# One sum of the experts' rows in memory split into two, with four row buffers

## The chip, the cores and the metric

The kernel runs on one core of one Trainium2 chip. A core has five engines that run side by side, each through its own list of instructions in order: PE (matrix products), DVE (VectorE, elementwise on whole tiles), ACT (ScalarE), POOL (GpSimd) and SP (which here only issues transfers). Sixteen DMA engines move data between the memory of the chip and the on-chip buffers; a transfer is issued by one of the engines into that engine's queue and reports its landing by a semaphore. The metric is the time of one execution on the device in microseconds.

## The reference

Two transformer blocks over 512 rows of 1024 numbers. The first ends in a mixture of 64 experts, of which a router picks eight for each row; a shared expert sees every row. What matters here:

```
scores = sigmoid(t @ router_w);  top_i = the 8 experts of a row;  top_w = their weights
x1     = x + gate1 * mixer(...)                    # residual, 512 x 1024
routed = sum over a row's experts e of top_w[e] * (silu(g) * u) @ w_dn[e],  [g, u] = t @ w_gu[e]
shared = (silu(g) * u) @ w_sh_dn
x2     = x1 + g2 * (routed + shared)               # g2: a gate per column
out    = second_block(rmsnorm(x2) * final_g, ...)
```

All is in 32-bit floats; `x2` is the sum that this change is about.

## The kernel before

The kernel is one class whose phases follow each other: A and B (the first block's mixer), C (the experts), D (the second block). Weights are streamed from memory: each of the 64 experts has 2 MB of up-projection in two pieces of 1 MB (`load_gu`) and 1 MB of down-projection (`load_dn`), issued by SP. Weights are split on the chip into a high part (ACT, line 166, `whi`) and a low part (DVE, line 167, `wlo`), and each product is made of three matmuls (lines 160 to 162).

Phase C first picks the experts of each row on DVE, and from these, by small matmuls, lists of row numbers (`iidx`) and weights (`widx`) for each expert. The experts are taken in a fixed order of slots, each with a fixed number of rows, `CAP[n]`: the first three have 128, then large and small ones take turns (88, 36, 88, 36 down to 68, 64), then come fourteen of up to 128, ending with 96, 96, 92, 92, 88 and 28. Rows beyond a slot's number would go through `overflow`, which runs only when there are some.

The loop in `phase_c` (line 1167 on) does for slot n: load the weights; turn the gathered rows (`ring`, four buffers) on PE, split them into `th` and `tl`, and multiply them (`routed_up`); gather the rows of slot n+4 by a transfer on POOL's queue (`gather`, line 1199); multiply slot n-1 by its down-projection (`routed_down`): eight matmuls, two `ps_dn` banks of 512 columns, then DVE multiplies by `g2` into a row buffer `ey` (line 1326), and POOL issues the scatter (line 1327), a transfer that adds each row of `ey` to its row of the sum `accd` in memory. `ey` has two buffers; the last two slots use two others (tag `th`). Transfers that add to one tensor must not overlap, so each scatter waits until the one before has landed, and a new `ey` waits until the scatter that reads its buffer has landed.

Before the loop, `shared_down` (lines 1002 to 1017) makes the shared expert's 512 x 1024 results in eight steps of 128 x 512: `sy` on DVE, then POOL adds it to the residual `x1`, and after a row block's second half POOL writes it to `accd`, which so starts as residual plus shared expert. `sy` and `ey` share two buffers.

After the loop, `moe_end` (line 1331) loads `accd` back in four transfers of 512 KB on SP (`mo`, line 1340), takes the sums of squares on ACT and the product with `final_g` on DVE (`fin`, line 1351), turns the rows on PE and makes the second block's first input (`hn`, line 1506).

The order of instructions on each engine is set when the kernel is built: a scheduler places them by its own estimate of times, together with marks in the code (`self.after(...)`), and buffers come from pools with a fixed number of each tag. The `hp` and `tok` areas that held early activations hold expert weights during the loop (n modulo 4 picks `wraw`, `hh`, `hl` or `tok`).

Of the kernel before, what the change touches and what calls it, by code (L numbers as in the profile page):

```python
# [8 lines left out]
F32 = mybir.dt.float32  # L9
# [6 lines left out]
OP = mybir.AluOpType  # L16
AX = mybir.AxisListType

S = 512
D = 1024  # L20
# [5 lines left out]
NE = 64  # L26
# [11 lines left out]
CAP = [SLOTS[r] for r in RANK]  # L38
# [103 lines left out]
class Kern:  # L142
# [859 lines left out]
    def shared_down(self):  # L1002

        nc, c = self.nc, self.cpool
        for half in range(2):
            cs = slice(half * 512, (half + 1) * 512)
            dh, dl = self.dn_piece(self.shd, half)
            for i in range(4):
                ahl = self.sha[i // 2]
                ps = self.bank("dn")  # L1010
                for k in range(2):
                    self.mm3(ps, ahl[:, 0, i % 2, k], ahl[:, 1, i % 2, k], dh[:, k], dl[:, k], k == 0, k == 1)
                y = c.tile([128, 512], F32, name="sy", tag="ey", bufs=2)
                nc.vector.tensor_tensor(y, ps, self.g2[:, cs], OP.mult)
                nc.gpsimd.tensor_tensor(self.x1[:, i, cs], self.x1[:, i, cs], y, OP.add)
                if half:
                    nc.gpsimd.dma_start(self.accd[i * 128:(i + 1) * 128, :], self.x1[:, i])

    def phase_c(self):
        nc, p, c = self.nc, self.p, self.cpool  # L1020
        hh, hl = self.hh, self.hl
        accd = self.dp.tile([S, D], F32, name="accd")
        self.mark = self.mark2 = self.mark3 = None

        self.onesb = c.tile([128, 128], BF, name="onesb")
# [14 lines left out]
        for n in range(4):  # L1040
            r = c.tile([128, D], F32, name=f"ring{n}", tag="ring", bufs=4)
# [124 lines left out]
        for n in range(NE):  # L1166
            if n % 2 == 0 and n + 6 < NE:
                with self.after(self.last):
                    self.slots(n + 6, 2, self.pos, self.RH)
            e = slice(n, n + 1) if n < FIRST else bass.ds(self.order_at(self.order[0:1, n:n + 1]), 1)  # L1170
            gu = self.load_gu(p["w_exp_gu"][0, e], n)
            dns.append(self.load_dn(p["w_exp_dn"][0, e], n))
            pg = self.routed_up(self.ring[n % 4], gu, CAP[n])
            if n + 4 < NE:
                self.gather(n + 4)
            if pend is not None:
                self.routed_down(*pend[1], dns[n - 1], self.iidx[:, n - 1:n], CAP[n - 1])
            pend = e, self.expert_act(pg, self.widx[:, n:n + 1], CAP[n], {NE - 2: "sco", NE - 1: "mk"}.get(n))
        self.routed_down(*pend[1], dns[NE - 1], self.iidx[:, NE - 1:NE], CAP[NE - 1])

        self.fin = self.raw()[:, 0:D]
        with self.after(self.loaded):
# [77 lines left out]
    def overflow(self):  # L1260

        nc, c, p, tc = self.nc, self.cpool, self.p, self.tc
        most = nc.values_load(self.cnt[0:1, 64:65], min_val=0, max_val=S)
        with tc.If(most > 0):
            with tc.For_i(0, NE, 1) as n:
                n_e = nc.values_load(self.cnt[0:1, bass.ds(n, 1)], min_val=0, max_val=S)
                with tc.If(n_e > 0):
                    e = bass.ds(self.order_at(self.order[0:1, bass.ds(n, 1)]), 1)
                    pos = c.tile([128, 4], F32, name="ovp", tag="ovp")
                    nc.vector.tensor_copy(pos, self.pos[:, :, bass.ds(n, 1)].rearrange("p i o -> p (i o)"))  # L1270
                    rh = c.tile([128, 4, 6], BF, name="ovr", tag="ovr")
                    nc.vector.tensor_copy(rh, self.RH[:, :, bass.ds(n, 1), :].rearrange("p i o n -> p (i o) n"))
                    cap = c.tile([128, 1], F32, name="ovc", tag="ovc")
                    nc.vector.tensor_copy(cap, self.cap[:, bass.ds(n, 1)])
                    nc.vector.tensor_scalar(pos, pos, cap, None, op0=OP.subtract)
                    for r in range(-(-(S - min(CAP)) // 128)):
                        if r:
                            nc.vector.tensor_scalar(pos, pos, -128.0, None, op0=OP.add)
                        ps = self.bank("sl")
                        self.slot_sums(ps[:, 0:6], pos, rh)  # L1280
                        wi = c.tile([128, 1], F32, name="ovw", tag="ovw")
                        ii = c.tile([128, 1], I32, name="ovi", tag="ovi")
                        self.slot_lists(ps, 1, wi, ii)
                        self.mark = self.mark2 = self.mark3 = None
                        gu, dn = self.load_gu(p["w_exp_gu"][0, e], 1), self.load_dn(p["w_exp_dn"][0, e], 1)
                        g = self.ring[0]
                        self.gather_rows(g, ii, 128)
                        self.routed_down(*self.expert_act(self.routed_up(g, gu, 128), wi, 128), dn, ii, 128)

    def routed_up(self, g, gu, m):  # L1290
        nc, c = self.nc, self.cpool
# [17 lines left out]
                    self.mark = mm  # L1309
        return pg  # L1310

    def routed_down(self, af, ah, al, dn, i_ap, m):
        nc, c = self.nc, self.cpool
        y = c.tile([128, D], F32, name="ey", tag="ey" if af is not None else "th", bufs=2)
        dv = dn[:].rearrange("p (k c) -> p k c", k=2)
        for half in range(2):
            cs = slice(half * 512, (half + 1) * 512)
            ps = self.bank("dn")
            if af is None:
                dh, dl = self.dn_piece(dn, half)  # L1320
                for k in range(2):
                    self.mark2 = self.mm3(ps[0:m], ah[:, k, 0:m], al[:, k, 0:m], dh[:, k], dl[:, k], k == 0, k == 1)
            else:
                for k in range(2):
                    self.mark2 = nc.tensor.matmul(ps[0:m], af[:, k, 0:m], dv[:, k, cs], start=k == 0, stop=k == 1)
            nc.vector.tensor_tensor(y[0:m, cs], ps[0:m], self.g2[0:m, cs], OP.mult)
        nc.gpsimd.indirect_dma_start(out=self.accd[:], in_=y[0:m], in_offset=None, compute_op=OP.add,
                                     out_offset=bass.IndirectOffsetOnAxis(ap=i_ap[0:m], axis=0),
                                     bounds_check=S - 1, oob_is_err=False)

    def moe_end(self, A, B):

        nc, p, d = self.nc, self.p, self.dpool
        area, fg = self.ap_.tile([128, 4, D], F32, name="fin", tag="tok"), self.fin
        ys = [self.m4.tile([128, D], F32, name="mo", tag=t, bufs=b) for t, b in (("macc", 3),) * 2 + (("mraw", 2),) * 2]
        self.xT = d.tile([128, KT, S], F32, name="xT")
        hh = self.hp.tile([128, KT, S], F32R, name="dhh", tag="hh")
        hl = self.hp.tile([128, KT, S], F32R, name="dhl", tag="hl")
        for i in range(4):
            nc.sync.dma_start(ys[i], self.accd[i * 128:(i + 1) * 128, :])  # L1340

        w = d.tile([128, 1], F32, name="sqw", tag="sqw", bufs=1)
        seq = [nc.scalar.sqrt(w, self.eps)]
# [2 lines left out]
        def sums(n):  # L1346
            y, z, i, ss = ys[n], area[:, n], n % 2, st[n // 2]
            junk = hl[:, 2 * n:2 * n + 2].rearrange("p k s -> p (k s)")
            with self.after(seq[-1]):
                seq.append(nc.scalar.activation(junk, y, AF.Square, accum_out=ss[:, i:i + 1]))  # L1350
            nc.vector.tensor_tensor(z, y, fg, OP.mult)
            with self.after(seq[-1]):
                seq.append(nc.scalar.activation(y, z, AF.Square, accum_out=ss[:, 2 + i:3 + i]))
# [34 lines left out]
        with self.tc.high_priority():  # L1388
            sums(0)
            sums(1)  # L1390
            first(0)
            turned(0)
            b0 = second(0)
            sums(2)
            sums(3)
            first(1)
            self.norm_half(0, A, B, b0[:, 0:256], hh, hl)
            with self.after(self.bcast):
                turned(1)
            b1 = second(1)  # L1400
            self.norm_half(1, A, B, b1[:, 0:256], hh, hl)
# [498 lines left out]
```

## Time and profile before

| what | us |
|---|---|
| median of three runs (lowest to highest) | 3308.69 (3306.46 to 3318.46) |
| the profiled execution's own time | 3290.82 |
| its span from first to last instruction | 3289.1 |
| PE busy in it | 3089.7 (94%) |
| DVE busy | 1922.6 (58%) |
| ACT busy | 1231.9 (37%) |
| POOL busy | 566.3 (17%) |

The profile is of one execution; its times count from the start of its span. PE is busy nearly throughout, so what matters is where it is not. The expert loop lies between about 600 and 1308 us; the second block starts after about 1350. The DMA share is the mean busy share of the sixteen DMA engines. A releaser ("<-") is what ended a wait. The granted clock (PEclk) is a share of TensorE's full speed.

### The profile page before, as it was taken

To read this page: it belongs to the slowest core of one execution; us is meant where nothing else is said; L and a number is where in the kernel's file an instruction comes from. 1 tells how busy PE (TensorE), PEld (TensorE's weight loads), DVE (VectorE), ACT (ScalarE), POOL (GpSimd) and SP (SyncE) were. 2 spreads that over 40 slices of the span, in tenths; PEclk is the share of its full clock that TensorE was granted. 3 is DMA by queue.
4 is the path that set the end of the run, shared out by engine and by line. 5 is a ranking of instruction groups with operands and counts; after the bars stand their busy time and mean duration, and the time that the engine had idled before them with its cause. 6 is when DMAs were issued, how large, how long until landed. Compare 5 with 4: busy or idle time off the path is not lost.

```text
span 3289.1 us, 40726 instructions
## 1 busy us (share of the span) xinstructions
PE 3089.7 (94%) x15632; PEld 2346.1 (71%) x15633; DVE 1922.6 (58%) x2958; ACT 1231.9 (37%) x1976; POOL 566.3 (17%) x374
## 2 busy tenths in 40 slices
PE   6998997999999888699999999999999999999999
PEld 5876475554444454577888697888877888788888
DVE  6777768776766666565337565333764356653335
ACT  5133453554544444422235442223422245442223
POOL 0255524223233322100001110000000010100001
PEclk9998998999999999799999999999999999999999
DMA  6554334988989897475234246232665233232223
GB/s 241 162 165 154 114 133 152 332 313 310 326 300 315 305 307 253 147 232 196 90 109 124 68 164 205 90 99 97 203 214 169 90 126 93 76 117 94 98 90 103
DMA packets 316712, 573.44 MB, mean 174 GB/s; under 512 B 49392, under 2 KB 251952, under 8 KB 291936
## 3 DMA queue, kind: packets, MB, share of 16 engines
q1 hardware_dynamic: 293424, 525.17, 47.0%
q0 software_dynamic: 21008, 43.51, 5.5%
q8 instruction: 125, 2.05, 0.3%
q10 hardware_dynamic: 2080, 2.10, 0.2%
q14 instruction: 75, 0.61, 0.1%
HBM read 549.79 MB, written 26.30 MB: 175 GB/s over the span
## 4 chain that ended last, share of the span: by engine, by line
PE 48%; DMA 7%; DVE 4%; issue 1%; ACT 1%; POOL 0%; SPq 0%; DVEq 0%; POOLq 0%; ACTq 0%
PE ps_fm L162 10%; PE ps_fm L161 9%; PE ps_fm L160 9%; DMA mraw<-in_w_mod_dram 6%; PE ps_dn L160 5%; PE ps_dn L162 5%; PE ps_dn L161 5%; DVE macc L195 2%; PE ps_dn L1760 1%; DMA accd<-ey,iidx 1%; DVE wlo L167 1%; PE ps_po L1787 1%; ACT whi L166 0%; PE ps_sm L1781 0%; PE ps_dn L1761 0%
## 5 line engine op out<-in xcount | busy, mean ns | idle before, releaser
L167 DVE TENSOR_TENSOR wlo<-wraw,whi 128x1024 fp32r<-128x1024 f32 x480 | 577.6, 1209 | 573.7 <-ACT whi L166 566.2
L166 ACT CAST whi<-wraw 128x1024 fp32r<-128x1024 f32 x480 | 486.8, 1018 | 847.6 <-PE ps_fm L161 367.9
L160 PE MATMUL ps_fm<-dhh,whi 128*128 128x512 f32 (+1 forms) x1808 | 676.9, 377 | 14.9 <-ACT whi L166 6.6
L162 PE MATMUL ps_fm<-dhh,wlo 128*128 128x512 f32 (+1 forms) x1808 | 668.5, 378 | 14.8 <-DVE wlo L167 14.6
L161 PE MATMUL ps_fm<-dhl,whi 128*128 128x512 f32 (+1 forms) x1808 | 676.3, 376 | 1.6 <-DVE dhl L1508 0.9
L162 PEld LDWEIGHTS ps_fm<-dhh,wlo 128*128 128x128 f32 x1808 | 342.2, 190 | 79.3 <-DVE wlo L167 18.4
L160 PEld LDWEIGHTS ps_fm<-dhh,whi 128*128 128x128 f32 x1808 | 341.0, 190 | 78.8 <-ACT whi L166 8.7
L161 PEld LDWEIGHTS ps_fm<-dhl,whi 128*128 128x128 f32 x1808 | 342.0, 190 | 63.8 <-DVE dhl L1508 3.5
L160 PE MATMUL ps_dn<-ah,whi 128*128 128x256 f32 (+1 forms) x1152 | 384.1, 335 | 1.5 <-DVE xT L1583 1.4
L162 PE MATMUL ps_dn<-ah,wlo 128*128 128x256 f32 (+1 forms) x1152 | 382.4, 334 | 0.0
L161 PE MATMUL ps_dn<-al,whi 128*128 128x256 f32 (+1 forms) x1152 | 382.2, 332 | 0.0
L167 DVE TENSOR_TENSOR wlo<-wbig,whi 128x1024 fp32r<-128x1024 f32 x192 | 231.5, 1217 | 112.0 <-ACT whi L166 111.9
L161 PEld LDWEIGHTS ps_dn<-al,whi 128*128 128x128 f32 x1152 | 217.0, 188 | 25.0 <-issue 1.5
L160 PEld LDWEIGHTS ps_dn<-ah,whi 128*128 128x128 f32 x1152 | 216.6, 188 | 24.9 <-DVE xT L1583 2.5
L166 ACT CAST whi<-wbig 128x1024 fp32r<-128x1024 f32 x192 | 197.3, 1047 | 97.6 <-PE ps_gu L162 50.8
L162 PEld LDWEIGHTS ps_dn<-ah,wlo 128*128 128x128 f32 x1152 | 216.1, 188 | 24.1 <-issue 0.8
L1470 POOL TENSOR_TENSOR sq<-sq 128x256 f32<-128x256 f32 x72 | 77.6, 1077 | 854.2 <-issue 719.8
L161 PE MATMUL ps_gu<-wlo,th 128*128 128x512 f32 (+21 forms) x512 | 208.7, 408 | 12.6 <-DVE wlo L167 12.3
L160 PE MATMUL ps_gu<-whi,th 128*128 128x512 f32 (+21 forms) x512 | 208.8, 409 | 3.6 <-ACT whi L166 3.5
L162 PE MATMUL ps_gu<-whi,tl 128*128 128x512 f32 (+21 forms) x512 | 202.4, 395 | 1.9 <-DVE tl L167 1.9
L195 DVE SCALAR_TENSOR_TENSOR macc<-mraw,cact,macc 128x1024 f32<-128x1024 f32 x105 | 134.7, 1283 | 101.2 <-DMA mraw<-in_w_mod_dram 100.7
L1583 DVE SCALAR_TENSOR_TENSOR xT<-ps_dn,modc,xT 128x256 f32<-128x256 f32 (+1 forms) x160 | 93.4, 587 | 157.7 <-PE ps_dn L162 156.3
(530 smaller groups left out, 4387.3 us busy)
## 6 DMA issues: line engine op xcount, KB each, us to landing
wbig<-in_w_exp_gu_dram SPq DMA_DIRECT2D x96, 1024.0 KB
wraw<-in_w_ffn_gu_dram SPq DMA_DIRECT2D x86, 1024.0 KB
mraw<-in_w_mod_dram SPq DMA_DIRECT2D x144, 512.0 KB
dnraw<-in_w_exp_dn_dram SPq DMA_DIRECT2D x48, 1024.0 KB
wraw<-in_w_exp_gu_dram SPq DMA_DIRECT2D x32, 1024.0 KB
wraw<-in_w_ffn_down_dram SPq DMA_DIRECT2D x32, 1024.0 KB
wraw<-in_w_out_dram SPq DMA_DIRECT2D x24, 1024.0 KB
wraw<-in_w_ffn_down_dram SPq DMA_DIRECT2D x32, 768.0 KB
```

What stands on the lines that cost most here:

```text
L160: mm(ps, ah, bh, start=first, stop=False)
L161: mm(ps, ah, bl, start=False, stop=False)
L162: return mm(ps, al, bh, start=False, stop=last)
L166: self.copied = self.nc.scalar.copy(hi, src)
L167: self.nc.vector.tensor_tensor(lo, src, hi.bitcast(F32), OP.subtract)
L195: nc.vector.scalar_tensor_tensor(acc, w, cact[:, k:k + 1], acc, op0=OP.mult, op1=OP.add)
L1470: nc.gpsimd.tensor_tensor(self.ssq, self.ssq, t, OP.add)
L1583: nc.vector.scalar_tensor_tensor(self.xT[:, k, hs], ps[j], G[:, k:k + 1], self.xT[:, k, hs], op0=OP.mult, op1=OP.add)
L1760: nc.tensor.matmul(ps[:, a], q[gp, t, t_], kk[gp, j0 * 128:(i + 1) * 128], start=True, stop=False)
L1787: nc.tensor.matmul(pso[b * 64:(b + 1) * 64, g * 256:(g + 1) * 256], v[:, j0 + j, gp], pts[j][:, b * 256:(b + 1) * 256], start=j == 0, stop ...
```

## The change

There are two tensors in memory, `acc0d` and `acc1d`. The first gets the residual `x1`, by four transfers of POOL at the head of `shared_down`; the second gets the shared expert: each `sy` is written there by POOL, eight transfers of 256 KB, and POOL's eight adds are gone. The scatter of slot n adds to `accd[n % 2]`. The row buffers of odd slots come from the pool `m4` (tag `macc`, of whose three buffers `g2` holds one), so that there are four. In `moe_end` SP loads row blocks of both sums in turn (`mo` and `mo2`, the latter in `hh`), and DVE adds the two before the sums of squares.

```diff
--- before.py
+++ after.py
@@ -1002,6 +1002,8 @@
     def shared_down(self):
 
         nc, c = self.nc, self.cpool
+        for i in range(4):
+            nc.gpsimd.dma_start(self.accd[0][i * 128:(i + 1) * 128, :], self.x1[:, i])
         for half in range(2):
             cs = slice(half * 512, (half + 1) * 512)
             dh, dl = self.dn_piece(self.shd, half)
@@ -1012,14 +1014,13 @@
                     self.mm3(ps, ahl[:, 0, i % 2, k], ahl[:, 1, i % 2, k], dh[:, k], dl[:, k], k == 0, k == 1)
                 y = c.tile([128, 512], F32, name="sy", tag="ey", bufs=2)
                 nc.vector.tensor_tensor(y, ps, self.g2[:, cs], OP.mult)
-                nc.gpsimd.tensor_tensor(self.x1[:, i, cs], self.x1[:, i, cs], y, OP.add)
-                if half:
-                    nc.gpsimd.dma_start(self.accd[i * 128:(i + 1) * 128, :], self.x1[:, i])
+                nc.gpsimd.dma_start(self.accd[1][i * 128:(i + 1) * 128, cs], y)
 
     def phase_c(self):
         nc, p, c = self.nc, self.p, self.cpool
         hh, hl = self.hh, self.hl
-        accd = self.dp.tile([S, D], F32, name="accd")
+
+        accd = [self.dp.tile([S, D], F32, name=f"acc{n}d") for n in range(2)]
         self.mark = self.mark2 = self.mark3 = None
 
         self.onesb = c.tile([128, 128], BF, name="onesb")
@@ -1174,9 +1175,9 @@
             if n + 4 < NE:
                 self.gather(n + 4)
             if pend is not None:
-                self.routed_down(*pend[1], dns[n - 1], self.iidx[:, n - 1:n], CAP[n - 1])
+                self.routed_down(*pend[1], dns[n - 1], self.iidx[:, n - 1:n], CAP[n - 1], n - 1)
             pend = e, self.expert_act(pg, self.widx[:, n:n + 1], CAP[n], {NE - 2: "sco", NE - 1: "mk"}.get(n))
-        self.routed_down(*pend[1], dns[NE - 1], self.iidx[:, NE - 1:NE], CAP[NE - 1])
+        self.routed_down(*pend[1], dns[NE - 1], self.iidx[:, NE - 1:NE], CAP[NE - 1], NE - 1)
 
         self.fin = self.raw()[:, 0:D]
         with self.after(self.loaded):
@@ -1285,7 +1286,7 @@
                         gu, dn = self.load_gu(p["w_exp_gu"][0, e], 1), self.load_dn(p["w_exp_dn"][0, e], 1)
                         g = self.ring[0]
                         self.gather_rows(g, ii, 128)
-                        self.routed_down(*self.expert_act(self.routed_up(g, gu, 128), wi, 128), dn, ii, 128)
+                        self.routed_down(*self.expert_act(self.routed_up(g, gu, 128), wi, 128), dn, ii, 128, r)
 
     def routed_up(self, g, gu, m):
         nc, c = self.nc, self.cpool
@@ -1309,9 +1310,12 @@
                     self.mark = mm
         return pg
 
-    def routed_down(self, af, ah, al, dn, i_ap, m):
+    def routed_down(self, af, ah, al, dn, i_ap, m, n):
         nc, c = self.nc, self.cpool
-        y = c.tile([128, D], F32, name="ey", tag="ey" if af is not None else "th", bufs=2)
+        if af is not None and n % 2:
+            y = self.m4.tile([128, D], F32, name="ey", tag="macc", bufs=3)
+        else:
+            y = c.tile([128, D], F32, name="ey", tag="ey" if af is not None else "th", bufs=2)
         dv = dn[:].rearrange("p (k c) -> p k c", k=2)
         for half in range(2):
             cs = slice(half * 512, (half + 1) * 512)
@@ -1324,7 +1328,7 @@
                 for k in range(2):
                     self.mark2 = nc.tensor.matmul(ps[0:m], af[:, k, 0:m], dv[:, k, cs], start=k == 0, stop=k == 1)
             nc.vector.tensor_tensor(y[0:m, cs], ps[0:m], self.g2[0:m, cs], OP.mult)
-        nc.gpsimd.indirect_dma_start(out=self.accd[:], in_=y[0:m], in_offset=None, compute_op=OP.add,
+        nc.gpsimd.indirect_dma_start(out=self.accd[n % 2][:], in_=y[0:m], in_offset=None, compute_op=OP.add,
                                      out_offset=bass.IndirectOffsetOnAxis(ap=i_ap[0:m], axis=0),
                                      bounds_check=S - 1, oob_is_err=False)
 
@@ -1334,10 +1338,12 @@
         area, fg = self.ap_.tile([128, 4, D], F32, name="fin", tag="tok"), self.fin
         ys = [self.m4.tile([128, D], F32, name="mo", tag=t, bufs=b) for t, b in (("macc", 3),) * 2 + (("mraw", 2),) * 2]
         self.xT = d.tile([128, KT, S], F32, name="xT")
+        zs = self.hp.tile([128, 4, D], F32, name="mo2", tag="hh")
+        for i in range(4):
+            for dst, src in ((ys[i], self.accd[0]), (zs[:, i], self.accd[1])):
+                nc.sync.dma_start(dst, src[i * 128:(i + 1) * 128, :])
         hh = self.hp.tile([128, KT, S], F32R, name="dhh", tag="hh")
         hl = self.hp.tile([128, KT, S], F32R, name="dhl", tag="hl")
-        for i in range(4):
-            nc.sync.dma_start(ys[i], self.accd[i * 128:(i + 1) * 128, :])
 
         w = d.tile([128, 1], F32, name="sqw", tag="sqw", bufs=1)
         seq = [nc.scalar.sqrt(w, self.eps)]
@@ -1346,6 +1352,7 @@
         def sums(n):
             y, z, i, ss = ys[n], area[:, n], n % 2, st[n // 2]
             junk = hl[:, 2 * n:2 * n + 2].rearrange("p k s -> p (k s)")
+            nc.vector.tensor_tensor(y, y, zs[:, n], OP.add)
             with self.after(seq[-1]):
                 seq.append(nc.scalar.activation(junk, y, AF.Square, accum_out=ss[:, i:i + 1]))
             nc.vector.tensor_tensor(z, y, fg, OP.mult)
```

On DVE, around the shared expert and the row lists, this is the order before; `sy` is a shared expert's result, `sel`, `wt`, `den`, `pos` and `RH` belong to the router and the lists.

```order
L1014 TENSOR_TENSOR sy<-ps_dn,g_4101 128x512
L1105 TENSOR_REDUCE den<-wt 128x4
L167 TENSOR_TENSOR wlo<-wraw,whi 128x1024
L1106 RECIPROCAL den<-den 128x4
L1014 TENSOR_TENSOR sy<-ps_dn,g_4101 128x512
L1212 SCALAR_TENSOR_TENSOR pos_4216<-ps_sl,sel 128x12
L1108 TENSOR_SCALAR wt<-wt,den 128x64 x4
L1214 TENSOR_SCALAR pos_4216<-pos_4216 128x12
L1014 TENSOR_TENSOR sy<-ps_dn,g_4101 128x512
```

After, on DVE at the end of that part; `perm` to `cnt` belong to the order of the experts, `tl` is the first routed expert's rows.

```order
L1137 TENSOR_SCALAR perm<-cpk,rank 64x64
L1158 CAST order<-ps_at 1x64
L1160 TENSOR_TENSOR cntf<-ps_at,cap 1x64
L1161 TENSOR_SCALAR cntf<-cntf 1x64
L1162 TENSOR_REDUCE cntf<-cntf 1x1
L1164 CAST cnt<-cntf 1x65
L1016 TENSOR_TENSOR sy<-ps_dn,g_4102 128x512 x6
L167 TENSOR_TENSOR wlo<-wraw,whi 128x1024
L1148 COPY sel<-ps_dn 128x256
L1149 CAST selb<-sel 128x256
L167 TENSOR_TENSOR tl<-ps_tr,th 128x512
```

Before, six `sy` stood one by one between the instructions of the router; now two come early and the other six stand together after `cnt`, ahead of `sel` and the first `tl`.

On POOL, the end of the shared expert and the first gathers before:

```order
L1015 TENSOR_TENSOR x_3288<-x_3288,sy 128x512 x5
L1017 DMA accd<-x_3288 128x1024
L1015 TENSOR_TENSOR x_3288<-x_3288,sy 128x512 x2
L1017 DMA accd<-x_3288 128x1024 x2
L1015 TENSOR_TENSOR x_3288<-x_3288,sy 128x512
L1199 DMA ring_4086<-h2d,iidx 128x1024
L1199 DMA ring_4088<-h2d,iidx 128x1024
L1199 DMA ring_4090<-h2d,iidx 128x1024
L1017 DMA accd<-x_3288 128x1024
```

And the same place of POOL after, through to the first two scatters:

```order
L1017 DMA acc1d<-sy 128x512 x2
L1200 DMA ring_4087<-h2d,iidx 128x1024
L1200 DMA ring_4089<-h2d,iidx 128x1024
L1200 DMA ring_4091<-h2d,iidx 128x1024
L1017 DMA acc1d<-sy 128x512 x6
L1200 DMA ring_4093<-h2d,iidx 88x1024
L1200 DMA ring_4087<-h2d,iidx 36x1024
L1200 DMA ring_4089<-h2d,iidx 88x1024
L1331 DMA acc0d<-ey,iidx 512x1024
L1331 DMA acc1d<-ey,iidx 512x1024
```

The adds are gone, the writes of the residual have moved up ahead of these rows, six writes of `sy` stand behind the first three gathers, and the scatters take the two tensors in turn, as they do to the end of the loop.

## Rows read from the trace of the kernel before

**Rows 1.** Windows: us; busy PE, PEld, DVE, ACT, POOL; PEclk, DMA share, GB/s.

```profile
640.00:720.00 80.00, 80.00 (x351) 41.84 (x349) 59.56 (x118) 39.05 (x62) 17.20 (x15) 1.00 0.96 348
798.00:908.00 110.00, 108.25 (x463) 54.75 (x462) 78.86 (x161) 53.44 (x80) 34.60 (x21) 1.00 0.96 328
940.00:1020.00 80.00, 71.67 (x280) 34.43 (x278) 48.62 (x102) 32.28 (x48) 30.05 (x13) 0.91 0.83 277
...
1080.00:1180.00 100.00, 88.22 (x373) 51.93 (x372) 66.71 (x133) 44.95 (x66) 33.35 (x15) 0.98 0.88 293
```

**Rows 2.** Waits of 940:1180: engine, waited for; total us, times, longest us.

```profile
POOL accd L1327 <- DMA accd<-ey,iidx: 31.3, 11, 6.1
...
DVE ey L1326 <- DMA accd<-ey,iidx: 25.7, 7, 4.6
...
PE ps_dn L1325 <- DVE ey L1326: 16.4, 7, 3.2
```

**Rows 3.** The tile `accd` in 790:910: durations ns, starts us; then landing.

```profile
L1327 POOL DMA_INDIRECT accd<-ey,iidx x11: 1396/1457/1834, 798.8 to 908.2; - x11
...
DMA to landing us min/median/max: 9.7/11.0/12.2
```

**Rows 4.** The tile `accd` in the whole span.

```profile
L1327 POOL DMA_INDIRECT accd<-ey,iidx x64: 1395/1599/4259, 597.3 to 1333.0; - x64
...
DMA to landing us min/median/max: 6.1/8.5/13.3
```

**Rows 5.** Chain of waits in 1284:1350: start us, us, what ran.

```profile
1299.78 1.92 DMA accd<-ey,iidx
1301.70 11.97 issue
...
1313.92 11.22 DMA accd<-ey,iidx
...
1325.96 6.21 DMA accd<-ey,iidx
...
1332.96 4.79 DMA accd<-ey,iidx
...
1339.16 7.99 DMA mo<-accd
```

**Rows 6.** Timeline of POOL in 1284:1345: start, us, instruction [idle before].

```profile
1293.69 1.45 POOL L1327 DMA_INDIRECT accd<-ey,iidx  x1 [5.00 <-issue]
```

**Rows 7.** Timeline of VectorE (DVE) in 1276:1310.

```profile
1286.12 1.28 DVE L1326 TENSOR_TENSOR ey<-ps_dn,g 96x512 f32<-96x512 f32 x2
...
1293.04 1.28 DVE L1326 TENSOR_TENSOR ey<-ps_dn,g 92x512 f32<-92x512 f32 x2 [2.25 <-DMA accd<-ey,iidx]
...
1298.99 1.28 DVE L1326 TENSOR_TENSOR ey<-ps_dn,g 92x512 f32<-92x512 f32 x2 [3.15 <-DMA accd<-ey,iidx]
...
1307.09 0.68 DVE L1326 TENSOR_TENSOR ey<-ps_dn,g 28x512 f32<-28x512 f32 x1 [0.25 <-PE ps_dn L162]
```

**Rows 8.** A window in which one scatter of 92 rows is alone.

```profile
1316.00:1324.00 8.00, 0.00 (x0) 0.00 (x0) 0.75 (x1) 0.39 (x1) 0.00 (x0) 0.50 0.25 40
```

**Rows 9.** Timeline of VectorE (DVE) in 540:580.

```profile
564.00 0.16 DVE L1258 TENSOR_TENSOR iidx<-slt,slu 128x3 int32<-128x3 f32 x1
...
567.65 0.42 DVE L1147 COPY sel<-ps_dn 128x256 f32<-128x256 f32 x1 [2.12 <-PE ps_dn L1146]
...
573.40 0.67 DVE L167 TENSOR_TENSOR tl<-ps_tr,th 128x512 fp32r<-128x512 f32 x1
```

**Rows 10.** DMA issues in 480:620: KB each, us from issue to landing.

```profile
h2d<-h POOLq DMA_DIRECT2D x4, 512.0 KB, 3.2
...
accd<-x POOLq DMA_DIRECT2D x4, 512.0 KB, 6.6
```

**Rows 11.** Timeline of VectorE (DVE) in 1338:1354.

```profile
1343.43 1.22 DVE L1351 TENSOR_TENSOR fin<-mo,wraw 128x1024 f32<-128x1024 f32 x1
...
1351.82 1.26 DVE L1506 SCALAR_TENSOR_TENSOR hn<-xT,modc,ps_sm 128x256 f32<-128x256 f32 x3 [2.17 <-PE ps_sm L1382]
```


## The prediction

> **What bounds the kernel now.** I read the windows over the expert loop first: TensorE (PE) is busy nearly without a gap wherever the weight transfers keep up, and the DMA engines run at 0.96 of their time in 640:720 and 798:908, with PE busy 80.00 of 80 and 108.25 of 110 us [rows 1]. So weights and matmuls are close to balanced, at a pace of (908.2-798.8)/10 = 10.94 us per expert between eleven scatters [rows 3]. Two stretches fall out: in 940:1020 PE is busy 71.67 of 80.00 us, at a granted clock of 0.91 (a mean between the levels of 1.2 and 2.4 GHz) and a DMA share of 0.83; in 1080:1180 it is 88.22 of 100.00, at 0.98 and 0.88 [rows 1]. When PE and DMA are both less than full, neither is the limit, so the next view was the waits of 940:1180: the scatters waited 31.3 us for the landing of the one before, VectorE's `ey` waited 25.7 us for a row buffer that a scatter still read, and PE waited 16.4 us for that `ey` to empty its bank [rows 2]. That is a chain scatter, buffer, bank, matmul. A scatter takes 6.1 to 13.3 us from issue to landing, median 8.5 [rows 4], against a pace of 10.94, and only one may be in flight.
>
> The chain of waits after the last matmuls shows it bare. VectorE ends the last expert's rows at 1307.09+0.68 = 1307.77 [rows 7], but the last scatter lands at 1332.96+4.79 = 1337.75 [rows 5]. In those 30.0 us nothing runs but scatters, one behind the other: expert 60's takes 1.92+11.97 us from its start at 1299.78, then 11.22 to the next entry, 6.21 and 4.79 [rows 5]. The loads of the sum start only then.
>
> **The change part by part.**
>
> *The first sum in two tensors, in the last scatters.* A scatter now waits for the one two earlier, and `ey` for the one four earlier. Going through the last ones with the old durations: 59's rows are there at 1286.12+1.28 = 1287.4 [rows 7], and its issue at 1293.69 [rows 6] moves to there, since it needs only 57. Before 60's rows VectorE waited 2.25 us, before 61's 3.15 [rows 7]; both waits go. 60 is then issued at about 1292, when its rows are written, and lands 13.9 us after that, 1306. 61's rows come about 2 us earlier than 1300.3, so it is issued at 1298 and lands, with the 11.22 us of its own old flight, at 1309.2. 62 needs 60: issued 1306, lands 6.2 later, 1312.2. 63 needs 61: issued 1309.2 and 4.8 more, 1314. The last landing moves from 1337.75 to 1314: **-24 us**. Bounds: -29 if the two in flight each take the median 8.5 and the end is again near the last `ey`; -18 if 61 takes 6 us longer because it shares engines with 60.
>
> What the row shows of sharing: while one 92-row scatter is alone, in 1316:1324, the DMA share is 0.25 at 40 GB/s [rows 8], that is 4 of 16 engines. The Trainium skill, page "DMA: Bandwidth & Descriptors", section "Why a DMA increments its semaphore by 16 and not by 1", says that a DMA is spread over the largest number up to 16 that divides its partition count, on consecutive engines from a cursor that moves on; 92 gives 4, which the 0.25 agrees with, and two in a row would stand on different engines. Its section "Queues, rings and completion order" adds that one engine takes the descriptors of one queue in their order, which speaks against the change wherever two scatters do meet on an engine. By the first rule the tail is -24, by the second at its worst nothing.
>
> *The same in the loop.* The waits of scatter on scatter and of `ey` on scatter go: with a pace of 10.94 us a scatter two earlier has 21.9 us to land, and the longest took 13.3 [rows 4]. What is late next is the weight transfer. I bound the gain twice. By PE: idle 8.33 us in 940:1020 and 11.78 in 1080:1180, and the low clock there, 0.09 of 80 and 0.02 of 100 = 9 us more, together 29 if all of it is these waits [rows 1]. By DMA: the share of 0.83 over 80 us and 0.88 over 100 going up to the 0.96 of the full stretches saves 80x(1-0.83/0.96) = 10.8 and 100x(1-0.88/0.96) = 8.3, together 19 [rows 1]; the bytes must be moved all the same. The lower bound rules, and some start-up of the pipeline is never full: **-16 us**, with 0 (the transfer had another reason for its gaps) and -29 as ends.
>
> *The shared expert.* Eight POOL adds go and eight writes of 256 KB come. The adds lay beside VectorE's routing work, so they save nothing; I cost their removal at 0. But `sy` has two buffers, and each from the third on must wait for a write to land. In the order six of them stand together behind `cnt`, ahead of the copy of `sel` and the first `tl` that PE's first routed matmuls need; everything behind them on VectorE waits too. Before, the six stood between routing instructions, with no wait on a transfer. `iidx` was ready at 564.00 [rows 9]; without the six ahead of it, about 0.68 us each as an `ey` of the same width [rows 7], that is 560, and `cnt` follows at about 563, since its matmuls no longer stand behind those of L1146. `sy` 3 and 4 go at once, 5 and 6 wait for their landing, 7 and 8 for that of 5 and 6: two round trips. A landing lies between 3.2 and 6.6 us, from 512 KB writes of the same queue in this stretch [rows 10]; I take the middle, 4.9, as half the bytes in the same traffic. With 0.7 for the instruction and, as an estimate, as much for the issue, 8 ends at 563+2x(4.9+1.4)+1.4 = 577, the first `tl` at 579 where it stood at 573.40 [rows 9]. Against these 6, the wait of 2.12 us before `sel` [rows 9] is covered: **+4 us** (-1 with landings of 3.2, +9 with 6.6). VectorE and PE are full right after, so a delay here passes on. The four writes of the residual stand far earlier on POOL, among the writes of `h2d`, where nothing waits for them: 0. The landing of all eight before the first odd scatter is hidden: the first scatter of all was issued at 597.3 [rows 4].
>
> *Loading both sums.* Instead of 2 MB, 4 MB are loaded after the last scatter. From its landing at 1337.75 the second `fin` began at 1343.43, and the first `hn` at 1351.82, 8.4 us later [rows 11]; the last of the old loads landed at 1339.16+7.99 = 1347.15, 9.4 us after the first issue [rows 5]. The first half of the rows now needs four loads, 2 MB, so their landing is the old last one, T0+9.4; one add of 1.22 us (the duration of `fin`, of the same shape [rows 11]) follows, then the same 8.4: `hn` at T0+19 instead of T0+14: **+5 us**. Bounds +3 (loads go faster when nothing else moves) and +9 (the second 2 MB take as long again, 8 us, and an add). The transfers of the sum that depend only on the first tensor could not start much earlier, because SP takes them in turn.
>
> Sum: -24-16+4+5 = **-31 us** on the profiled execution, 3290.8 us (span 3289.1). The median of the runs shown is 3308.7, 0.5% above it; the difference lies in no place that the change touches, so I take the same -31 there: **3278 us**.
>
> **Rivals.**
>
> *Only the tail.* The gaps of the loop have another cause, for instance prefetch buffers that come free late. For it: most waits of the scatter in 940:1180 end elsewhere than on a scatter. Against: PE waits 16.4 us for `ey` and `ey` 25.7 for scatters, the same chain [rows 2]. Then -24+4+5 = -15: 3294.
>
> *The scatters queue behind each other on their engines.* All go through POOL's one queue; if two in flight meet on the same engines, the second lands when it would have. Then the wait moves from POOL to the landing; the row buffers still help the loop by perhaps 8, the tail gives only the gaps between the entries of the chain, some 2 [rows 5]: -2-8+9 = -1, 3308. Against: 0.25 of the engines at a time leaves room [rows 8].
>
> *Two scatters in flight slow the weights* (the other side). In the stretches at 0.96 the loop is held by transfers [rows 1], and there a scatter takes 9.7 to 12.2 us, nearly the pace [rows 3]. Two at a time on a few engines hold back the share of every weight piece on those engines, and a piece is there when its last share is. Each microsecond per expert costs 64 us; it turns the -31+16 = -15 into slower than before by 0.5% from (15+16.5)/64 = 0.5 us per expert; with 0.75 it is -15+48 = +33: 3342. Against it: the bytes are the same, and with one scatter in flight nearly all of the time the stretch already is as crowded.
>
> *All gaps go*, -29 in the loop: 3265.
>
> **How the numbers follow.** Differences under 0.5%, 16.5 us, count as no change, about what a measurement of this kernel can tell. The forecast has 0.66, its own range 3266 to 3291 (the four terms' ends, not all at once); all gaps gone 0.05; only the tail 0.15; queueing 0.08; slower weights 0.06. Faster: 0.61 of the forecast, 0.05, and 0.06 of the tail case, which lies just short of the limit: 0.72; slower 0.06; the rest, 0.22, no change. The range for 8 in 10 takes in most of the tail case and part of the all-gaps case: 3257 to 3303.
>
> **What would show it.** In the profile after: no wait of POOL's scatter on the scatter before it in 940:1180, `ey` there without a wait on a scatter, PE's busy time in these windows like that of 798:908, and a DMA share at 0.96. In the tail overlapping scatters, and 20 to 28 us between the last `ey` and the first load shrunk to under 10. `sy` with two waits on its writes, of 3 to 7 us, and the first `tl` some us later; `hn` about 19 us after the first load. Wrong would be: a scatter's landing much longer than 13.3 us when two are in flight, windows of weights with a pace above 11 us, or `sy` waits that add over 10 us.

## The result, and the profile after

The changed kernel takes 3269.1 us (median; 3268.3 to 3271.8) against 3307.6 for the kernel before: a ratio of 0.9879, 95% interval 0.9856 to 0.9903, or 38.5 us less. The profiled execution of after took 3271.8 us (span 3270.0), 19 us less than the profiled one of before. The forecast was 3278, in a range of 3257 to 3303.

To place the change, both traces are cut at the same instructions. "sy" is the start of the first shared-expert result, "ey" the start of a routed expert's rows (the first, and the second half of the last), "load" the issue of the first load of the sum, "hn" the first input of the second block; times are lengths in us between them.

| kernel | first sy at | to first ey | to last ey | to load | to hn | sy to hn |
|---|---|---|---|---|---|---|
| before | 542.9 | 47.0 | 717.2 | 30.7 | 14.0 | 808.9 |
| after | 550.5 | 61.6 | 684.4 | 16.3 | 17.9 | 780.2 |
| difference | +7.6 | +14.5 | -32.7 | -14.4 | +3.9 | -28.7 |

The 7.6 us ahead of the first `sy` are not the change's: the stages before it hold the same work, and a second execution of before (b0 below) begins `sy` at 550.3. From there to the second block's first input the profiles differ by -28.7 us (-26.7 to the end of the span), where -31 was forecast; but the parts differ from the forecast by much more than the sum does.

In the loop the chain of [rows 2] is gone. Windows as in [rows 1] (columns: us; busy PE, PEld, DVE, ACT, POOL; PEclk; DMA share; GB/s), after:

```profile
640.00:720.00 80.00, 80.00 (x336) 40.23 (x334) 61.42 (x122) 38.23 (x59) 19.18 (x15) 1.00 0.97 339
798.00:908.00 110.00, 108.08 (x462) 56.46 (x462) 79.57 (x159) 53.25 (x82) 27.47 (x18) 0.97 0.89 310
940.00:1020.00 80.00, 80.00 (x347) 41.21 (x344) 59.60 (x121) 38.72 (x59) 27.00 (x16) 1.00 0.96 337
1080.00:1180.00 100.00, 96.49 (x421) 58.35 (x420) 74.92 (x145) 50.73 (x74) 32.76 (x19) 1.00 0.99 332
```

PE is busy 80.00 of 80 and 96.49 of 100 us in the two stretches that had fallen out, at full granted clock (2.4 GHz), and the DMA share is 0.96 and 0.99. Of the waits of after in 940:1180, these are the longest and, behind them, all of more than half a microsecond in which a scatter of POOL is the one that waits:

```profile
ACT eaf L971 <- PE ps_at L967: 81.1, 22, 3.9
POOL ring L1200 <- issue: 76.9, 10, 8.0
...
POOL acc1d L1331 <- issue: 3.7, 11, 0.7
...
POOL acc0d L1331 <- DVE oh L1243: 2.4, 8, 0.3
...
POOL acc0d L1331 <- DVE tl L167: 0.6, 2, 0.3
```

No scatter waits for a scatter there, and no row has `ey` waiting for one. POOL stands idle 76.9 us ahead of its gathers (`ring`) without a releaser that the profile shows; PE, busy as above, is not held up by it.

The start is late, on DVE in 556:600 (start, us, instruction, [idle before <- releaser]):

```profile
564.36 1.27 DVE L1016 TENSOR_TENSOR sy<-ps_dn,g 128x512 f32<-128x512 f32 x2
575.84 0.69 DVE L1016 TENSOR_TENSOR sy<-ps_dn,g 128x512 f32<-128x512 f32 x1 [10.21 <-DMA acc1d<-sy]
578.01 0.69 DVE L1016 TENSOR_TENSOR sy<-ps_dn,g 128x512 f32<-128x512 f32 x1 [1.48 <-DMA acc1d<-sy]
581.99 1.30 DVE L1016 TENSOR_TENSOR sy<-ps_dn,g 128x512 f32<-128x512 f32 x2 [3.29 <-DMA acc1d<-sy]
...
588.03 0.42 DVE L1148 COPY sel<-ps_dn 128x256 f32<-128x256 f32 x1 [3.62 <-PE ps_dn L1147]
...
589.76 0.69 DVE L167 TENSOR_TENSOR tl<-ps_tr,th 128x512 fp32r<-128x512 f32 x1 [0.97 <-ACT th L166]
```

Behind `cnt`, the first pair of `sy` runs at once, then DVE stands 10.21, 1.48 and 3.29 us for the landing of the writes of earlier ones, and the first `tl` starts at 589.76; [rows 9] had it at 573.40, so from the first `sy` it comes 39.3 us instead of 30.5, 8.8 later. A further wait on these writes stands on ACT, and PE waits for what ACT writes there:

```profile
585.40 0.58 ACT L1144 COPY sT<-ps_tr 64x512 f32<-64x512 f32 x1 [3.23 <-DMA acc1d<-sy]
586.03 1.97 PE L1147 MATMUL ps_dn<-perm,sT 64*128 64x64 f32 x8 [4.95 <-ACT sT L1144]
```

Between the first `tl` and the first `ey` 22.3 us pass instead of 16.5. PE's granted clock there was between its levels of 1.2 and 2.4 GHz for a time, where before it was full; columns as above, after and then before:

```profile
590.00:601.00 11.00, 11.00 (x55) 9.28 (x55) 8.57 (x22) 4.70 (x6) 0.00 (x0) 0.69 0.21 62
```

```profile
573.40:584.00 10.60, 9.88 (x56) 8.24 (x57) 9.06 (x19) 6.77 (x9) 0.00 (x0) 1.00 0.77 293
```

The tail, POOL in 1230:1340:

```profile
1273.73 2.18 POOL L1331 DMA_INDIRECT acc1d<-ey,iidx  x1 [7.84 <-DVE ey L1330]
1284.12 4.90 POOL L1331 DMA_INDIRECT acc0d<-ey,iidx  x1 [8.21 <-DVE ey L1330]
1289.33 1.94 POOL L1331 DMA_INDIRECT acc1d<-ey,iidx  x1 [0.30 <-issue]
1304.43 1.60 POOL L1331 DMA_INDIRECT acc0d<-ey,iidx  x1 [13.17 <-DMA acc0d<-ey,iidx]
1306.34 2.05 POOL L1331 DMA_INDIRECT acc1d<-ey,iidx  x1 [0.30 <-DVE wlo L167]
```

61's scatter is issued right behind 60's, 5.2 us later, as forecast; before, they were 14.1 us apart [rows 5]. But 60's takes until 1304.3 to land, 20.2 us, and 62 waits 13.17 us for it. From the last `ey` to the first load it is 16.3 us, not the "under 10" that the prediction named as a sign. And the second block's start, DVE:

```profile
1318.09 1.23 DVE L1355 TENSOR_TENSOR mo<-mo,mo 128x1024 f32<-128x1024 f32 x1 [9.83 <-DMA mo<-acc1d]
1319.35 1.23 DVE L1358 TENSOR_TENSOR fin<-mo,wraw 128x1024 f32<-128x1024 f32 x1
1321.45 1.22 DVE L1355 TENSOR_TENSOR mo<-mo,mo 128x1024 f32<-128x1024 f32 x1 [0.88 <-DMA mo<-acc1d]
1322.71 1.22 DVE L1358 TENSOR_TENSOR fin<-mo,wraw 128x1024 f32<-128x1024 f32 x1
...
1330.67 1.27 DVE L1513 SCALAR_TENSOR_TENSOR hn<-xT,modc,ps_sm 128x256 f32<-128x256 f32 x3 [1.25 <-PE ps_sm L1389]
```

The add of the second row block (L1355) starts at 1321.45, 8.6 us after the first load at 1312.8, and `hn` at 17.9 us after it; in [rows 11] it was 14.0.

### The profile page after: what moved, and what is told of

Same layout as the page of the kernel before. It is cut to its first block, busy times and chain, and to the rows that moved or that the text cites. A ratio compares the mean times of both kernels' runs of the same rounds, so it can differ in the third digit from the quotient of the medians.

```text
span 3270.0 us, 40750 instructions
## 1 busy us (share of the span) xinstructions
PE 3091.5 (95%) x15632; PEld 2356.4 (72%) x15633; DVE 1929.4 (59%) x2962; ACT 1232.5 (38%) x1976; POOL 542.8 (17%) x374
## 4 chain that ended last, share of the span: by engine, by line
PE 71%; DMA 12%; DVE 9%; issue 4%; POOL 2%; ACT 2%; SPq 0%; DVEq 0%; POOLq 0%; ACTq 0%
PE ps_fm L162 9%; PE ps_fm L160 9%; PE ps_fm L161 9%; DMA mraw<-in_w_mod_dram 7%; PE ps_dn L1329 5%; PE ps_dn L160 5%; PE ps_dn L162 5%; PE ps_dn L161 5%; PE ps_gu L160 3%; PE ps_gu L161 3%; PE ps_gu L162 3%; DVE macc L195 2%; PE ps_tr L1299 2%; DMA wraw<-in_w_exp_gu_dram 2%; DVE wlo L167 1%
## 5 line engine op out<-in xcount | busy, mean ns | idle before, releaser
L162 PEld LDWEIGHTS ps_fm<-dhh,wlo 128*128 128x128 f32 x1808 | 341.7, 190 | 80.8 <-DVE wlo L167 20.2
L161 PE MATMUL ps_gu<-wlo,th 128*128 128x512 f32 (+21 forms) x512 | 210.4, 411 | 11.2 <-DVE wlo L167 11.2
## 6 DMA issues: line engine op xcount, KB each, us to landing
wbig<-in_w_exp_gu_dram SPq DMA_DIRECT2D x96, 1024.0 KB, 13.9
wraw<-in_w_exp_gu_dram SPq DMA_DIRECT2D x32, 1024.0 KB, 13.3
```

The costliest lines, as they stand in the source:

```text
L161: mm(ps, ah, bl, start=False, stop=False)
L162: return mm(ps, al, bh, start=False, stop=last)
```

## The experiments

**b0, the kernel before once more.**

> The kernel before once more, for a second profile. The profiled execution of before was 18 us below the median of its timed runs, that of the change was not. If the executions of before differ in the expert loop (its scatters wait for each other by more or less): from the first sy to the first load of the sum it takes 800 to 815 us instead of 795. If they differ in the stages before it: 795 us again and another time of the first sy.

Measured: 3302.5 us, span 3300.7; first `sy` at 550.3, first load at 1344.4: 794.1 us between them, against 794.9 in the first profile. So the executions of before differ ahead of this stage (and a few us behind it), and the sections of the table can be compared. It does not explain all of the distance: timed runs of before have medians of 3308 to 3313 us, its two profiled ones took 3291 and 3303.

**e1, only the four row buffers.** The change's two edits to `y` in the kernel before, with one sum:

```diff
-        y = c.tile([128, D], F32, name="ey", tag="ey" if af is not None else "th", bufs=2)
+        if af is not None and n % 2:
+            y = self.m4.tile([128, D], F32, name="ey", tag="macc", bufs=3)
+        else:
+            y = c.tile([128, D], F32, name="ey", tag="ey" if af is not None else "th", bufs=2)
```

> One sum in memory as before, only the four row buffers of the change. If the row buffers carry the gain of the loop (VectorE no longer waits for a scatter to free its buffer, while POOL may still wait for the scatter before): the waits of ey on scatters in 940:1180 (25.7 us before) go, the loop gains 20 to 29 us, the last chain of scatters stays at about 30 us: 3280 to 3290 us. If the two sums carry it: less than 8 us gained, 3300 to 3308.

Measured: 3313.2 us, ratio 1.0016 (1.0001 to 1.0031): no gain. The waits in 940:1180 (total us, times, longest):

```profile
POOL accd L1330 <- DMA accd<-ey,iidx: 85.7, 16, 11.2
...
DVE ey L1329 <- DMA accd<-ey,iidx: 18.4, 6, 4.9
...
PE ps_dn L1328 <- DVE ey L1329: 10.3, 4, 3.5
```

and the end of its POOL:

```profile
1312.92 1.92 POOL L1330 DMA_INDIRECT accd<-ey,iidx  x1 [4.97 <-DMA accd<-ey,iidx]
1325.21 1.93 POOL L1330 DMA_INDIRECT accd<-ey,iidx  x1 [10.37 <-DMA accd<-ey,iidx]
1337.23 1.60 POOL L1330 DMA_INDIRECT accd<-ey,iidx  x1 [10.08 <-DMA accd<-ey,iidx]
1344.23 1.39 POOL L1330 DMA_INDIRECT accd<-ey,iidx  x1 [5.40 <-DMA accd<-ey,iidx]
```

POOL's wait of scatter on scatter grows from 31.3 [rows 2] to 85.7 us: the buffers only let the rows queue up ahead of the one scatter in flight, and `ey` still waits 18.4 us. The queue is paid back at the end, where from the last `ey` to the load it is 40.2 us instead of 30.7. What limited the loop was how many scatters can be served in a time, not how many rows can be held.

**e2, two sums and two row buffers.** After, with `y` as in the kernel before (both from `ey`).

> The change with two sums, but two row buffers. If the scatters' wait for each other is what holds the buffers: with a scatter issued as soon as its rows are there it has about 20 us to land before its buffer is wanted, so nothing waits and the time is that of the change, 3266 to 3275 us. If four buffers are needed: ey waits for scatters again by 20 us or more in 940:1180, and the time is 3285 to 3300.

Measured: 3272.8 us, ratio 0.9874 (0.9845 to 0.9902), 684.9 us from first to last `ey`: the same as the change. The two sums carry the gain; the third and fourth buffer add nothing that can be told. `ey` still waits for scatters, 5.7 us in 940:1180, too little to cost.

**e3, the shared expert to the first sum, zeros in the second.**

```diff
-        for i in range(4):
-            nc.gpsimd.dma_start(self.accd[0][i * 128:(i + 1) * 128, :], self.x1[:, i])
...
-                nc.gpsimd.dma_start(self.accd[1][i * 128:(i + 1) * 128, cs], y)
+                nc.gpsimd.tensor_tensor(self.x1[:, i, cs], self.x1[:, i, cs], y, OP.add)
+                if half:
+                    nc.gpsimd.dma_start(self.accd[0][i * 128:(i + 1) * 128, :], self.x1[:, i])
...
+        for i in range(4):
+            nc.gpsimd.dma_start(accd[1][i * 128:(i + 1) * 128, :], self.ring[3])
```

The last two lines stand in `phase_c`, behind the instruction that fills `ring` with zeros.

> The change, but the shared expert is added to the residual on POOL as before and both go into the first sum; the second sum starts as zeros, written early. If the round trips of sy on its writes delay the first experts (the first ey came 22 us later than before, 14.5 of them after the first sy): the loop starts 11 to 15 us earlier and the time is 3253 to 3260 us. If the weight transfers make that up in the loop anyway: 3266 to 3271, as the change.

Measured: 3264.7 us (3262.1 to 3272.1), ratio 0.9863 (0.9835 to 0.9892). From first `sy` to first `ey` 50.5 us instead of 61.6, to last `ey` 681.1, so 14.4 us come back by then in the profile; the timed medians differ by 4.5 us only, and their intervals overlap. By its own expectation the run lies between the two cases. The start alone is shown; how much of it reaches the end, e6 asks again.

**e6, `sy` in four buffers.** After, with every second `sy` from the pool `m4`:

```diff
-                y = c.tile([128, 512], F32, name="sy", tag="ey", bufs=2)
+                if i % 2:
+                    y = self.m4.tile([128, 512], F32, name="sy", tag="macc", bufs=3)
+                else:
+                    y = c.tile([128, 512], F32, name="sy", tag="ey", bufs=2)
```

> The change, with sy taken in turn from four buffers instead of two. If the first experts are late because sy waits for its own writes: the six sy wait once instead of twice, the time from the first sy to the first ey falls from 61.6 to 50 to 55 us, and the median is 3259 to 3266 us. If the landing of the writes is only an effect of the traffic and something else is late: 61 us and 3269.

Measured: 3259.4 us (3254.2 to 3259.9), ratio 0.9843 (0.9815 to 0.9871); 51.0 us from first `sy` to first `ey`, and 750.7 from first `sy` to the load (747.7 in e3), against 762.3 in after. No `sy` waits for a write any more; the order on DVE changed with the buffers, so that four `sy` come early instead of two. `sT` still waits, 6.6 us. So it was the two buffers, and about 10 us of the late start do reach the end: 9.7 by the timed medians, 11.6 at the load by the profiles (the intervals of the two ratios overlap, but no run of e6 is above 3259.9 us and none of after below 3268.3).

**e4, the row numbers 92, 76 and 68 rounded up, in the kernel before.** This asks whether the scatter's own length, not its order, was the trouble. One sum, two buffers:

```diff
-... [96] * 2 + [92] * 2 + ... [76] * 4 + ... [68] * 5 + ...
+... [96] * 2 + [96] * 2 + ... [80] * 4 + ... [72] * 5 + ...
```

> The kernel before, with the experts' row numbers 92, 76 and 68 rounded up to 96, 80 and 72, so that no scatter is spread over four engines only; one sum, two buffers. If the slow scatters on four engines are what made the waits: landings stay under about 9 us, the waits of ey on scatters in 940:1180 fall from 25.7 to under 8 us, the last chain shortens by 8 to 14 us, 3270 to 3285 us. If the spread over engines is not the cause: 3300 to 3308.

Measured: 3268.9 us (3264.4 to 3269.9), ratio 0.9868 (0.9842 to 0.9893): as much as the whole change, by 11 numbers in a table, and just under the range that was expected for that case. Of the landings, expected under 9 us, its profile holds too few to tell. The only wait on a scatter left in 940:1180, and the end of POOL:

```profile
POOL accd L1327 <- DMA accd<-ey,iidx: 4.8, 3, 2.6
```

```profile
1276.87 2.16 POOL L1327 DMA_INDIRECT accd<-ey,iidx  x1 [10.01 <-DVE ey L1326]
1283.53 2.17 POOL L1327 DMA_INDIRECT accd<-ey,iidx  x1 [4.50 <-DMA accd<-ey,iidx]
1290.62 1.42 POOL L1327 DMA_INDIRECT accd<-ey,iidx  x1 [4.91 <-issue]
1300.47 1.59 POOL L1327 DMA_INDIRECT accd<-ey,iidx  x1 [8.43 <-DMA accd<-ey,iidx]
1307.45 1.38 POOL L1327 DMA_INDIRECT accd<-ey,iidx  x1 [5.39 <-DMA accd<-ey,iidx]
```

60's and 61's scatters, now of 96 rows, take 7.1 and 9.9 us from issue to the next issue; with 92 rows they took 14.1 and 12.0 [rows 5]. The second profile of before (b0), which has the landing of every scatter, shows it for all: from the fourth expert of the loop on, the eleven with 92, 76 and 68 rows land after a median of 15.3 us (11.2 to 17.6), the other fifty after 8.7 (3.7 to 13.2). The rule of the Trainium skill that the prediction used (page "DMA: Bandwidth & Descriptors", section "Why a DMA increments its semaphore by 16 and not by 1") gives 4 engines for 92, 76 and 68 rows, 16 for 96 and 80 and 12 for 72; the traces agree in that the long scatters are those with the first three numbers, and in that the DMA share is 0.25 beside a lone one of 92 rows [rows 8] and 0.50, at 70 GB/s, beside the lone one of 88 rows behind it (1327:1331). Which engines move a scatter is not seen. The gathers of these experts take the same row numbers and change with them; but in b0 PE waits for gathers 0.2 us in all of 590:1320, so the gain is not theirs.

**e5, e3 with the rounded numbers, and e7, e6 with them.**

> The version with the shared expert added to the residual on POOL and a second sum of zeros, and with the row numbers 92, 76 and 68 rounded up to 96, 80 and 72. If the spread of a scatter over its engines is what the two sums work around, both together add little in the loop, and only the last chain gets shorter, by 4 to 8 us: 3256 to 3262 us. If they are two independent gains: 3225 to 3240.

> The change with sy in four buffers and the row numbers 92, 76 and 68 rounded up to 96, 80 and 72. If the rounding works on the last chain and the loop whatever the start looks like: the last ey to the first load of the sum takes 7 to 10 us instead of 17, and the median is 3238 to 3248 us, as with the sum of zeros. If the gain of the rounding belonged to the other start: 3256 to 3262.

Measured: e5 3244.2 us (3238.3 to 3249.4), ratio 0.9805 (0.9779 to 0.9830); e7 3248.2 us, ratio 0.9807 (0.9792 to 0.9822). Both beat the changed kernel, by 25 and 21 us, the two alike within their intervals; e5 lies between the two cases of its expectation, so the gains neither add up in full nor stand in for each other. POOL at the end of e5:

```profile
1250.16 2.16 POOL L1333 DMA_INDIRECT acc1d<-ey,iidx  x1 [7.87 <-DVE ey L1332]
1260.50 4.42 POOL L1333 DMA_INDIRECT acc0d<-ey,iidx  x1 [8.19 <-DVE ey L1332]
1265.25 1.42 POOL L1333 DMA_INDIRECT acc1d<-ey,iidx  x1 [0.33 <-DVE eal L167]
1270.74 1.59 POOL L1333 DMA_INDIRECT acc0d<-ey,iidx  x1 [4.07 <-DVE eal L167]
1274.42 1.38 POOL L1333 DMA_INDIRECT acc1d<-ey,iidx  x1 [2.08 <-DMA acc1d<-ey,iidx]
```

62 follows 60 after 10.2 us instead of 20.3 in after, though POOL's instruction for 60 still takes 4.42 us, and from the last `ey` to the load it is 8.2 us, in e7 8.4. In the middle of the loop the median landing of a scatter shows the same (transfer, queue, count, median us to landing; 940:1180), after and then e5:

```profile
acc0d<-ey,iidx POOLq DMA_INDIRECT x11, 15.0
acc1d<-ey,iidx POOLq DMA_INDIRECT x11, 17.3
```

```profile
acc0d<-ey,iidx POOLq DMA_INDIRECT x11, 9.0
acc1d<-ey,iidx POOLq DMA_INDIRECT x11, 9.8
```

The parts of all kernels, cut as above:

| kernel | first sy to first ey | to last ey | to load | to hn | sum | timed median, ratio |
|---|---|---|---|---|---|---|
| b0 (before) | 47.0 | 718.0 | 29.1 | 12.8 | 806.9 | 3302.5 (one run) |
| e1 buffers | 49.2 | 715.6 | 40.2 | 13.7 | 818.7 | 3313.2, 1.0016 |
| e2 sums | 61.5 | 684.9 | 17.2 | 19.8 | 783.4 | 3272.8, 0.9874 |
| e3 zeros | 50.5 | 681.1 | 16.1 | 18.9 | 766.6 | 3264.7, 0.9863 |
| e6 four sy | 51.0 | 682.8 | 17.0 | 18.5 | 769.2 | 3259.4, 0.9843 |
| e4 rounded | 49.1 | 689.1 | 19.0 | 14.4 | 771.6 | 3268.9, 0.9868 |
| e5 zeros, rounded | 50.5 | 676.3 | 8.2 | 18.6 | 753.6 | 3244.2, 0.9805 |
| e7 four sy, rounded | 52.7 | 677.6 | 8.4 | 19.9 | 758.6 | 3248.2, 0.9807 |

## Why the prediction was right, and where its steps were not

The direction, the place of the gains and the time were right; three of the four terms were mis-sized, and their errors cancelled. That the sum of the parts came within 3 us is luck.

*The loop, -16 forecast, -32.7 measured.* The mechanism was right (e1 and e2: it is the scatters' wait for each other, not the number of buffers). The size failed at the step "by DMA", which ruled over "by PE": it took the transfers' bound from two windows only. A window of before that it passed over had slack in the transfers without a gap on PE:

```profile
720.00:798.00 78.00, 77.01 (x342) 39.75 (x341) 59.08 (x126) 39.61 (x60) 25.04 (x15) 1.00 0.82 287
```

The whole loop, from the first `ey` to the end of the last, before and then after:

```profile
589.94:1307.77 717.83, 676.87 (x2852) 360.28 (x2850) 495.53 (x970) 333.66 (x499) 219.01 (x122) 0.99 0.91 308
```

```profile
612.06:1297.16 685.10, 666.73 (x2846) 361.69 (x2844) 498.27 (x968) 333.21 (x498) 200.68 (x123) 1.00 0.94 323
```

By these rows the same working gives 717.8x(1-0.91/0.96) = 37 us for the transfers, so they were not the tighter bound. PE's idle time fell from 41.0 to 18.4 us, and its busy time by 10.1 at a slightly higher granted clock: together 32.7. The bound by PE, 29 from two windows, was near. The late start did not help the loop: e3, which starts its experts 11 us earlier, needs 681.1 us, still less.

*The last scatters, -24 forecast, -14.4 measured*, outside the stated ends of -18 to -29. (About 2 of the 24 us are 61's earlier rows, which the table counts in the loop: by its cut -18 and -22 were forecast for the two.) The order of issue came as forecast; the failed step is "with the old durations". 60's flight took 20.2 us instead of 13.9. Its POOL instruction alone took 4.90 us instead of 1.92; the DMA share in 1284.2:1289.0 was 0.00, so the rows moved only when it had ended. Then 60 ran beside 61, which took 15.4 us to land instead of 11.2. The forecast had allowed up to 6 us for sharing, on 61 alone. The chain of 60 and 62 set the end. e3 and e5, which differ in the row numbers alone, show that these made most of the length: from 60's issue to 62's 20.2 and 10.2 us.

*The shared expert, +4 forecast, +14.5 to the first `ey`.* The two round trips were there, but the first landing cost DVE 10.21 us where 3.2 to 6.6 had been taken for it from [rows 10]: the bound came from writes at other moments, and here three gathers had just been issued ahead on POOL's queue, beside the weights (that these made it long was not tried). And a further wait was overlooked: `sT`, which PE needs for `sel`, is in the same two buffers, and ACT waited 3.23 us for a write to land. The sign named against the forecast, "`sy` waits that add over 10 us", came true: they add 15. At the first `tl` 8.8 of the 14.5 us are there. The other 5.8 come behind it and had no term: PE, idle 4.95 us for `sT` until 586.03, then had a granted clock of 0.69 in 590:601; as an estimate from that row, 11x(1-0.69) = 3.4 us. (The stated ends of this term, -1 and +9, do not come out of its own sum either: with landings of 3.2 and 6.6 it gives about +0.6 and +7.4.) e3 and e6 take about 10 of the 14.5 back in the start, and keep 12 to 15 us at the load.

*Loading both sums, +5 forecast, +3.9 measured.* Right.

*The rivals.* "Only the tail" falls: the loop gave the larger part. "The scatters queue behind each other" falls as forecast there, though 60's long flight has something of it. "Two scatters in flight slow the weights" falls: single scatters did get longer in the loop, from a median of 11.0 us in b0 to 15.0 and 17.3 in 940:1180, but the pace did not suffer, because nothing waited for them: from scatter 27 to 41 it is 10.7 us per expert, where before it was 11.9. And e5, with two in flight too, has 9.0 and 9.8, so it is not two in flight as such. The 13.3 us named as a sign against the forecast could not tell: it was the longest of the 14 landings, of 64, that the first profile of before holds, and b0, with one in flight, has up to 17.6.

What the prediction missed as a whole: the waits it counted were the consequence of eleven long scatters, those of 92, 76 and 68 rows. It had the row for that [rows 8] and used it only to argue that two of them fit beside each other; and of the 14 landings behind the median of 8.5 us [rows 4] one was such a scatter's. e4 removes the cause with one sum, and gains as much.

Open stays some 10 us: the medians of after and before differ by 38.5 us, the profiles from the first `sy` to `hn` by 28.7 (27 against b0). Both profiles of before took less than the medians of its timed runs, by 5 to 22 us; where its other executions lose that was not seen. Open too is why POOL's instruction for 60 is so long.

## What to carry to other kernels

When transfers that must not overlap stand in a chain, ask first why each of them is long, and only then how many may be in flight: here 4 rows more on 11 experts did as much as a second sum with its 2 MB of loads. More buffers ahead of a serial server only move the queue to the end (e1). When a change lets a transfer write from a buffer that a busy engine refills, count every tenant of that buffer's tag and price the landing under the traffic of that moment, not by a write at another moment.

## What the runs showed of the hardware

- From its issue to the next one in the serial chain a scatter of 92 rows took 14.1 and 12.0 us, one of 96 rows in the same place (e4) 7.1 and 9.9, one of 88 rows 7.0 [rows 5]. With one in flight (b0), scatters of 92, 76 and 68 rows landed after a median of 15.3 us, all others from the fourth on after 8.7; with these rounded up (e5), the same eleven after 9.4.
- POOL's instruction for a scatter took 1.4 to 2.4 us in most cases, but 4.90 us for expert 60 in after and 4.42 in e5, at the same place of the program, and 4.22 to 4.26 us five times in the loop of before; the cause was not tried.
- Executions of one kernel differ by up to 20 us in their timed runs (before: 3299 to 3319), and its two profiled ones by 7.4 us already before the first `sy`, at granted clocks of 0.85 and 0.74 in 240:320.
